# Four spectrum rows a block: one 1024-column product in place of two, and what storing them takes

## The chip, the cores and the metric

One Trainium2 chip; the program runs on one of its cores. The metric is the device time of one execution, in microseconds (us), lower is better. Three executions of the kernel before were timed, and one more was profiled. The engines are named as in the profile: PE is TensorE (PEld its weight loads), DVE is VectorE, ACT is ScalarE, POOL is GpSimd, and SP is the engine whose queue issues nearly all of the DMAs here.

## The reference, cut to what matters

One layer: a norm, a joint projection of 1024 tokens, three branches (Hyena long convolution, FNet, mLSTM), a merge and a mixture of experts. The change lies in the Hyena branch: the implicit filter is evaluated, turned into a spectrum, and multiplied with the spectrum of the signal, twice (order 0 and 1).

```python
def hyena_filter(L, lp):
    ...
    fwd, bwd = h[:, :, 0], h[:, :, 1]
    k = jnp.concatenate([fwd, jnp.zeros_like(fwd[:1]), jnp.flip(bwd[1:], axis=0)], axis=0)
    k = k * lax.rsqrt(jnp.sum(k * k, axis=0, keepdims=True) + EPS)
    return jnp.fft.rfft(k, axis=0)

def fft_longconv(u, kf, skip):
    L = u.shape[1]
    uf = jnp.fft.rfft(u, n=2 * L, axis=1)
    y = jnp.fft.irfft(uf * kf[None], n=2 * L, axis=1)[:, :L]
    return y + u * skip
...
    z = x1 * fft_longconv(v, kf[:, 0], skip[0])
    return x2 * fft_longconv(z, kf[:, 1], skip[1])
```

The product `uf * kf` is the complex product in question: re·re − im·im and re·im + im·re.

## The kernel before, in words

The transforms are matrix products with cosine and sine matrices, each float32 product done as three matmuls (`mm3`, lines L230 to L232) on a high and a low part of both factors; the parts come from a cast on ACT (L215) and a subtraction on DVE (L216). The program runs on one core as a line of stages, in us of the profiled span: about 0 to 200 start, conditioning and the filter's small network; 200 to 300 the **filter spectra**, interleaved with the projection; on to 650 the projection; then mLSTM and FNet; 880 to 1100 the **convolution**; merge, output and experts to the end.

`filt_spectra` goes over four kinds of spectrum in the order 2, 0, 1, 3 (kinds 0 and 1: real and imaginary part of the even frequencies, 2 and 3 of the odd ones), and in each over blocks of 128 frequencies (`fb`) and the two orders `o`. A kind loads its two folded filters (`kf<-pd`, 1 MB each) and the matrices (`fm`), splits them, and for each block and order runs a group of matmuls into PSUM (`pb`). From there come tiles `kk` of 128x512, in one of two ways: a block alone is copied out by ACT (L648); a pair of blocks is copied in one half by ACT (`ke`, L662) and combined by DVE to a sum (L664) and a difference (L665). Each tile is written to DRAM (`Kd`), L651 or L667. Row 0 of the first block of kind 0 carries two frequencies: in one place the halved value (L650) is wanted, in another a value that a small product gives (L627 to L631), which goes to a tensor of its own, `Kl` (L632). The tiles `kk` turn round in a ring of four buffers, so a fifth tile waits until the first one's write has landed.

In the convolution four passes (order, half of the channels) go over eight blocks each: four of even and four of odd frequencies (`par`, `fb`). `conv_fwd` makes a block's spectrum in PSUM (`p`, 128x2x256, real and imaginary), loads the filter's block with two DMAs (L956) and forms the product on DVE: one product with the tile as it is (L970), one with its two halves swapped (L971, a reversed view), a difference (L973), a sum (L974). In the first block of a pass (even, `fb` 0) the swapped tile is loaded by itself, with three DMAs: 128 rows (L966), rows 1 to 127 (L967), and row 0 from `Kl` (L968). `conv_inv` then transforms back, one block later.

Which instruction stands where on its engine is set by a scheduler when the kernel is built: from priorities, buffer rings and estimated durations it writes one fixed order for each engine, and each engine runs its list in that order. An instruction that waits holds up all that stand behind it on its engine; DMAs that SP issues stand in one such list, the filter's writes and the loads of the projection's weights alike.

Of the kernel before, what the change touches and what calls it, by code (L numbers as in the profile page):

```python
# [8 lines left out]
F32 = mybir.dt.float32  # L9
# [155 lines left out]
class Prog:  # L165
# [421 lines left out]
    def filt_spectra(self):  # L587
        nc = self.nc
        A = self.A

        self.Kd = self.dram([4, 4, 128, 2, 512], name="Kd")
        self.Kl = self.dram([1, 2, 512], name="Kl")

        skip = self.t("F2", "sk", 1, F32, (1, 2, 512))
        nc.sync.dma_start(skip.rearrange("p o c -> p (o c)"), self.skd.rearrange("i p -> (i p)").unsqueeze(0))
        for kind in (2, 0, 1, 3):
            kd, minus = {}, []
            for o in range(2):
                f = self.load("F2", "kf", 2, self.pd[o, kind].rearrange("k p c -> p k c"), (128, 4, 512))
                if kind < 2:  # L600

                    g, (a, b) = self.t("F2", "kf", 2, F32, (128, 4, 512)), (f[:, :2], f[:, 2:])
                    for i, sub in enumerate((kind == 1, kind == 0)):
                        (nc.vector.tensor_sub if sub else nc.vector.tensor_add)(g[:, 2 * i:2 * i + 2], a, b)
                    if kind == 0:
                        minus.append(self.t("F2", "kv", 2, F32, (1, 512)))
                        nc.vector.tensor_add(minus[o], g[0:1, 2, :], skip[:, o, :])
                        nc.sync.dma_start(g[0:1, 2, :], self.pv[o])
                        nc.vector.tensor_add(g[0:1, 2, :], g[0:1, 2, :], skip[:, o, :])
                        nc.vector.tensor_add(g[0:1, 0, :], g[0:1, 0, :], skip[:, o, :])  # L610
                    else:
                        nc.vector.tensor_copy(g[0:1, 2, :], f[0:1, 2, :])
                    f = g
                elif kind == 2:
                    nc.vector.tensor_add(f[0:1, 0, :], f[0:1, 0, :], skip[:, o, :])
                kd[o] = h, l = [self.t("F2", "kd" + x, 2, F32R, f.shape) for x in "hl"]
                for b in (0, 2):
                    self.split(h[:, b:b + 2], l[:, b:b + 2], f[:, b:b + 2])
            if kind == 0:
                p = self.ps("pb", (128, 2, 512))  # L620
                minus1 = self.t("F2", "sign", 1, F32R, (128, 2))
                nc.gpsimd.memset(minus1.bitcast(F32), -1.0)
                sign = self.onesr[:, :2], minus1
                for o in range(2):
                    h, l = kd[o]
                    for k in range(2):
                        nc.tensor.matmul(p[:2, o, :], sign[k], h[:, k, :], start=k == 0, stop=False)  # L627
                        nc.tensor.matmul(p[:2, o, :], sign[k], l[:, k, :], start=False, stop=k == 1)
                for o in range(2):
                    t = self.t("F2", "kk", 4, F32, (1, 512))  # L630
                    nc.vector.tensor_scalar(t, p[0:1, o, :], 0.5, None, op0=ALU.mult)  # L631
                    nc.sync.dma_start(self.Kl[:, o, :], t)  # L632
            for fb in (0, 2, 1) if kind < 2 else (0, 1):
                if kind == 0 and fb == 1:

                    for o in range(2):
                        self.split(kd[o][0][0:1, 0, :], kd[o][1][0:1, 0, :], minus[o])
                src = A["filt_odd"][kind - 2, fb] if kind > 1 else A["filt_even"][kind, fb]
                n = src.shape[1]
                mh, ml = self.parts("F2", "fm", 2, self.load("F2", "fm", 1, src, (128, n, 128)))  # L640
                if kind < 2 and fb < 2:
                    p = self.ps("pb", (128, 2, 512))
                    for o in range(2):
                        h, l = kd[o]
                        for k in range(2):
                            self.mm3(p[:, o, :], mh[:, k, :], ml[:, k, :], h[:, k, :], l[:, k, :], k == 0, k == 1)
                        kk = self.t("F2", "kk", 4, F32, (128, 512))
                        nc.scalar.copy(kk, p[:, o, :])  # L648
                        if kind == 0 and fb == 0:
                            nc.vector.tensor_scalar(kk[0:1], kk[0:1], 0.5, None, op0=ALU.mult)  # L650
                        nc.sync.dma_start(self.Kd[kind, fb, :, o, :], kk)  # L651
                    continue

                for o in range(2):
                    h, l = kd[o]
                    p = self.ps("pb", (128, 2, 512))
                    for i in range(2):
                        ks = [(k, k if kind > 1 else 2 + k) for k in range(i, n, 2)]
                        for k, kx in ks:
                            self.mm3(p[:, i, :], mh[:, k, :], ml[:, k, :], h[:, kx, :], l[:, kx, :], k == i, k == ks[-1][0])  # L660
                    e = self.t("F2", "ke", 1, F32, (128, 512))
                    nc.scalar.copy(e, p[:, 0, :])  # L662
                    kk = [self.t("F2", "kk", 4, F32, (128, 512)) for _ in range(2)]
                    nc.vector.tensor_add(kk[0], p[:, 1, :], e)  # L664
                    nc.vector.tensor_sub(kk[1], *((p[:, 1, :], e) if kind % 2 else (e, p[:, 1, :])))  # L665
                    for i in range(2):
                        nc.sync.dma_start(self.Kd[kind, fb + i * (2 if kind > 1 else 1), :, o, :], kk[i])  # L667
        if "kd" in self.dbg:
            nc.sync.dma_start(self.dbg["kd"], self.Kd)
            nc.sync.dma_start(self.dbg["kl"], self.Kl)  # L670
            nc.sync.dma_start(self.dbg["hnorm"], self.hnorm)


    def wblock(self, src):
# [234 lines left out]
    def conv_in(self, src, half, tiles=None, engines="vv"):  # L909


        nc = self.nc
# [16 lines left out]
        sh = (128, 2, 256)  # L929
        u2 = []  # L930
        for k in (0, 2, 1, 3):
# [6 lines left out]
            nc.scalar.copy(raw[k], p)  # L938
            if k >= 2:
                a, b = raw[k - 2], raw[k]  # L940
                e = [self.t("C", "t", 5, F32, sh) for _ in range(2)]
                nc.vector.tensor_add(e[0], a, b)
                nc.vector.tensor_sub(e[1], a, b)
                u2.append([self.parts("C", "u2", 4, e[i]) for i in range(2)])
        return u2, [raw[k] for k in range(4)]

    def conv_fwd(self, ut, o, half, par, fb):

        nc = self.nc
        cc = slice(256 * half, 256 * half + 256)  # L950
        if par and fb == 0:
            ut[1] = [self.parts("C1", "u1", 4, r) for r in ut[1]]
        p = self.ps("gp", (128, 2, 256))
        kk = self.t("C", "kk", 3, F32, (128, 2, 256))
        for im in range(2):
            nc.sync.dma_start(kk[:, im, :], self.Kd[2 * par + im, fb, :, o, cc])  # L956
            mh, ml = self.mat("f", par, im, fb)
            us = ut[1] if par else [u[im ^ (fb > 1)] for u in ut[0]]
            sg, nk = par ^ im, len(us)
            for k, (uh, ul) in enumerate(us):  # L960
                self.mm3(p[:, im, :], mh[:, k, :], ml[:, k, :], uh[:, sg, :], ul[:, sg, :], k == 0, k == nk - 1)
        sw = kk[:, ::-1, :]
        if par == 0 and fb == 0:

            sw = self.t("C", "t", 5, F32, (128, 2, 256))
            nc.sync.dma_start(sw[:, 0, :], self.Kd[1, 0, :, o, cc])  # L966
            nc.sync.dma_start(sw[1:128, 1, :], self.Kd[0, 0, 1:128, o, cc])  # L967
            nc.sync.dma_start(sw[0:1, 1, :], self.Kl[:, o, cc])  # L968
        t1, t2 = self.t("C", "t", 5, F32, (128, 2, 256)), self.t("C", "t", 5, F32, (128, 2, 256))
        nc.vector.tensor_mul(t1, p, kk)  # L970
        nc.vector.tensor_mul(t2, p, sw)  # L971
        y = self.t("C", "t", 5, F32, (128, 2, 256))
        nc.vector.tensor_sub(y[:, 0, :], t1[:, 0, :], t1[:, 1, :])  # L973
        nc.vector.tensor_add(y[:, 1, :], t2[:, 0, :], t2[:, 1, :])  # L974
        return self.parts("C", "y", 3, y)

    def conv_inv(self, acc, y, o, half, par, fb):


        nc = self.nc  # L980
# [17 lines left out]
        for g in range(2):  # L998
            for ct in range(2):
                i = 4 * o + 2 * half + ct  # L1000
                n, m = self.hnorm[:, i:i + 1], self.hnegn[:, i:i + 1]
                p = acc[0][g][ct]
                e = self.t("C1", "e", 1, F32, (128, 256))
                s = acc["s"][g][ct] = self.t("C1", "s", 4, F32, (128, 512))

                odd, even = (p[:, 256:], p[:, :256])[::1 if g == 0 else -1]
# [4 lines left out]
    def conv_out(self, acc, o, half, dst):  # L1011
# [7 lines left out]
        for part in range(2):  # L1019
            for ct in range(2):  # L1020
                i = 4 * o + 2 * half + ct
                if part == 0:
# [4 lines left out]
                    if o and half:  # L1027
                        nc.vector.scalar_tensor_tensor(s, acc[1][1][ct], n, s, op0=ALU.mult, op1=ALU.add)
                        continue
                    g = self.t("C", "t", 5, F32, (128, 512))  # L1030
                    nc.scalar.activation(g, acc[1][1][ct], AF.Copy, scale=n)
                    nc.vector.tensor_add(s, s, g)
                    continue
# [1126 lines left out]
```

## Time and profile before

| | |
|---|---|
| timed executions | 1688.49, 1693.48, 1694.13 us; median 1693.48 us |
| profiled execution | 1690.53 us, its span 1688.8 us |
| mean granted TensorE clock | 0.972 |
| busy shares of the span | PE 92%, DVE 71%, ACT 40%, POOL 19% |
| the chain that ended last | PE 73%, DVE 12%, DMA 8%, ACT 3% |

The busy shares are means over stages with different limits. The chain that ended last is followed back from the last instruction, from each instruction to what released it; a share of it tells on what kind of work the end of the program hung. The rows on which the argument rests are shown further down, in groups.

### The profile page before, as it was taken

How to read it: one execution, taken by the hardware profiler on the slowest of the kernel's cores; microseconds unless marked ns; L12 is line 12 of the kernel's file. 1: busy time of each engine (PE TensorE's matmuls, PEld its weight loads, DVE VectorE, ACT ScalarE, POOL GpSimd, SP SyncE). 2: the span in 40 equal slices, each digit the busy share in tenths (PEclk: the TensorE clock that was granted, in tenths of full speed). 3: DMA queues.
4: the chain of work that ended last, by engine and by line, in shares of the span. 5: the costliest groups of instructions: out<-in, count | busy, mean ns of one | idle time of the engine just before them, and what ended most of it. 6: DMA issues, size and time to landing. Idle time of an engine off the chain costs nothing.

```text
span 1688.8 us, 22676 instructions
## 1 busy us (share of the span) xinstructions
PE 1559.7 (92%) x8473; PEld 1300.7 (77%) x8473; DVE 1191.5 (71%) x1849; ACT 678.7 (40%) x1029; POOL 315.7 (19%) x282
## 2 busy tenths in 40 slices
PE   3999999999999999899989888899999969999993
PEld 1488877788888887778877777778878859999992
DVE  5689775966776869788645988864255567776776
ACT  4475545433222124444324433332033354554553
POOL 0000000000000001000002200125623354465651
PEclk9999999999999999999999999999999969999997
DMA  7544566422222365976435323585463388999984
GB/s 267 178 138 175 206 218 227 150 81 83 100 112 82 131 256 172 315 259 226 155 128 168 122 100 105 187 304 190 156 227 113 137 247 245 307 286 278 278 228 172
DMA packets 124355, 317.03 MB, mean 188 GB/s; under 512 B 18009, under 2 KB 40529, under 8 KB 124242
## 3 DMA queue, kind: packets, MB, share of 16 engines
q1 hardware_dynamic: 111562, 278.72, 47.8%
q0 software_dynamic: 10496, 32.36, 7.8%
q10 hardware_dynamic: 2184, 4.47, 0.7%
q8 instruction: 68, 1.11, 0.3%
q14 instruction: 45, 0.37, 0.1%
HBM read 226.49 MB, written 89.01 MB: 187 GB/s over the span
## 4 chain that ended last, share of the span: by engine, by line
PE 73%; DVE 12%; DMA 8%; ACT 3%; issue 3%; POOL 1%; SPq 0%; ACTq 0%; POOLq 0%; DVEq 0%
PE gp L230 12%; PE gp L231 11%; PE gp L232 11%; PE pb L230 8%; PE pb L232 8%; PE pb L231 8%; PE ph L230 2%; PE ph L232 2%; PE ph L231 2%; PE q L344 2%; DMA t<-Kl 1%; PE pb L1734 1%; DVE t L971 1%; DMA w<-sum 1%; DVE t L970 1%
## 5 line engine op out<-in xcount | busy, mean ns | idle before, releaser
L230 PE MATMUL gp<-ht,wh 128*128 128x512 f32 x784 | 310.6, 396 | 2.7 <-ACT wh L215 1.6
L232 PE MATMUL gp<-ht,wl 128*128 128x512 f32 x784 | 308.7, 394 | 0.9 <-DVE wl L216 0.9
L231 PE MATMUL gp<-ht,wh 128*128 128x512 f32 x784 | 309.0, 394 | 0.0
L230 PEld LDWEIGHTS gp<-ht,wh 128*128 128x128 f32 x784 | 148.4, 189 | 37.0 <-issue 2.3
L232 PEld LDWEIGHTS gp<-ht,wl 128*128 128x128 f32 x784 | 148.2, 189 | 31.7 <-DVE wl L216 1.3
L231 PEld LDWEIGHTS gp<-ht,wh 128*128 128x128 f32 x784 | 148.3, 189 | 30.9 <-DVE r L526 0.9
L230 PE MATMUL pb<-xh,gh 128*128 128x224 f32 x512 | 142.8, 279 | 0.0
L232 PE MATMUL pb<-xh,gl 128*128 128x224 f32 x512 | 141.8, 277 | 0.0
L231 PE MATMUL pb<-xl,gh 128*128 128x224 f32 x512 | 140.7, 275 | 0.0
L723 DVE SCALAR_TENSOR_TENSOR u<-z,hy_cw,u 128x945 f32<-128x945 f32 (+2 forms) x96 | 117.3, 1221 | 13.5 <-ACT u L715 11.3
L216 DVE TENSOR_TENSOR wl<-w,wh 128x1024 fp32r<-128x1024 f32 x57 | 70.4, 1235 | 63.5 <-ACT wh L215 63.1
L215 ACT CAST wh<-w 128x1024 fp32r<-128x1024 f32 x57 | 59.8, 1048 | 128.8 <-PE gp L231 82.0
L230 PEld LDWEIGHTS pb<-xh,gh 128*128 128x128 f32 x512 | 99.3, 194 | 0.3 <-ACT xh L215 0.2
L231 PEld LDWEIGHTS pb<-xl,gh 128*128 128x128 f32 x512 | 99.3, 194 | 0.1
L232 PEld LDWEIGHTS pb<-xh,gl 128*128 128x128 f32 x512 | 99.2, 194 | 0.0
L723 DVE SCALAR_TENSOR_TENSOR u<-z,ml_cw,u 128x945 f32<-128x945 f32 (+2 forms) x64 | 77.9, 1220 | 26.0 <-ACT u L715 24.9
L708 ACT ACTIVATE z<-gp,b_cols 128x512 f32<-128x512 f32 x48 | 32.8, 684 | 139.0 <-PE gp L232 139.0
L216 POOL TENSOR_TENSOR ml<-m,mh 128x512 fp32r<-128x512 f32 x24 | 34.9, 1454 | 194.8 <-ACT mh L215 191.6
L873 POOL MEMSET z<- 128x1024 f32 x1 | 1.0, 960 | 364.3 <-DVE u L723 364.3
L708 ACT ACTIVATE z<-gp,bh 128x512 f32<-128x512 f32 x46 | 31.6, 686 | 87.6 <-PE gp L232 74.7
L1690 POOL DMA_INDIRECT sum<-y,sidx x26 | 45.4, 1745 | 80.5 <-DVE y L1799 76.8
L1718 DVE TENSOR_TENSOR gl<-x,gh 128x1024 fp32r<-128x1024 f32 x33 | 40.4, 1230 | 28.1 <-ACT gh L1716 28.1
(608 smaller groups left out, 3972.6 us busy)
## 6 DMA issues: line engine op xcount, KB each, us to landing
w<-in_ada_rest SPq DMA_DIRECT2D x32, 512.0 KB
w<-in_w_gu SPq DMA_DIRECT2D x32, 512.0 KB
x<-in_w_gu SPq DMA_DIRECT2D x32, 512.0 KB
w<-in_w_gate SPq DMA_DIRECT2D x24, 512.0 KB
g<-gd SPq DMA_DIRECT2D x24, 512.0 KB
gd<-z SPq DMA_DIRECT2D x23, 512.0 KB
r<-in_ada_in SPq DMA_DIRECT2D x16, 512.0 KB
pd<-ft SPq DMA_DIRECT2D x32, 256.0 KB
```

The costliest lines, as they stand in the source:

```text
L215: self.copied = nc.scalar.copy(hi, src)
L216: return (nc.vector if eng == "v" else nc.gpsimd).tensor_sub(lo, src, hi.bitcast(F32))
L230: mm(ps, lh, rh, start=start, stop=False)
L231: mm(ps, lh, rl, start=False, stop=False)
L232: mm(ps, ll, rh, start=False, stop=stop)
L344: nc.tensor.matmul(p, c[:, kk, :], x[:, 512 * j:512 * j + 512], start=kk == 0 and x is ws[0], stop=kk == 7)
L708: return lambda s, p: self.nc.scalar.activation(z[:, s], p, func, bias=bias, scale=scale)
L723: last = nc.vector.scalar_tensor_tensor(ui[:, r0:r1, c0:c1], zi[:, r0 + dy:r1 + dy, c0 + dx:c1 + dx], taps[:, i:i + 1], ui[:, r0:r1, c0:c1 ...
L970: nc.vector.tensor_mul(t1, p, kk)
L971: nc.vector.tensor_mul(t2, p, sw)
L1690: return self.nc.gpsimd.indirect_dma_start(out=out, out_offset=bass.IndirectOffsetOnAxis(ap=ix, axis=0), in_=src, in_offset=None, **kw)
L1718: lo = (nc.vector if engines[i] == "v" else nc.gpsimd).tensor_sub(ml, m, mh.bitcast(F32))
```

## The change

Every block's spectrum is kept in DRAM as four rows of 256 for each half of the channels: re, −im, im, re. A function `keep` writes each `kk` tile twice, a real tile to rows 0 and 3, an imaginary one to row 2, and, negated by ACT into a further tile of the same ring, to row 1. Each write takes 128 rows of two pieces of 256. For kind 0, block 0, the write to row 3 leaves out row 0 of the frequencies (127 rows), since there the value that went to `Kl` before is written, now into `Kd` itself. In the convolution a block's four rows come with one DMA (128x1024), one DVE operation multiplies them with the spectrum in PSUM, read twice by a broadcast view, and one addition of 512 columns makes real and imaginary part of the product. The three extra loads of the first block are gone, and so is `Kl`. The ring `t` of the convolution goes from five tiles to four, and the small tile `e` moves into it.

```diff
-        self.Kd = self.dram([4, 4, 128, 2, 512], name="Kd")
-        self.Kl = self.dram([1, 2, 512], name="Kl")
+        self.Kd = self.dram([2, 4, 128, 2, 2, 4, 256], name="Kd")
+        def keep(kk, kind, fb, o):
+            par, im = divmod(kind, 2)
+            d = lambda i, a=0: self.Kd[par, fb, a:, o, :, i, :]
+            v = kk.rearrange("p (h c) -> p h c", h=2)
+            if not im:
+                nc.sync.dma_start(d(0), v)
+                a = int(kind == 0 and fb == 0)
+                nc.sync.dma_start(d(3, a), v[a:])
+                return
+            nc.sync.dma_start(d(2), v)
+            kn = self.t("F2", "kk", 4, F32, (128, 512))
+            nc.scalar.mul(kn, kk, -1.0)
+            nc.sync.dma_start(d(1), kn.rearrange("p (h c) -> p h c", h=2))
...
-                    nc.sync.dma_start(self.Kl[:, o, :], t)
+                    nc.sync.dma_start(self.Kd[0, 0, 0:1, o, :, 3, :], t.rearrange("p (h c) -> p h c", h=2))
...
-                        nc.sync.dma_start(self.Kd[kind, fb, :, o, :], kk)
+                        keep(kk, kind, fb, o)
...
-                        nc.sync.dma_start(self.Kd[kind, fb + i * (2 if kind > 1 else 1), :, o, :], kk[i])
+                        keep(kk[i], kind, fb + i * (2 if kind > 1 else 1), o)
...
-                e = [self.t("C", "t", 5, F32, sh) for _ in range(2)]
+                e = [self.t("C", "t", 4, F32, sh) for _ in range(2)]
...
-        kk = self.t("C", "kk", 3, F32, (128, 2, 256))
+        kk = self.t("C", "kk", 3, F32, (128, 2, 2, 256))
+        nc.sync.dma_start(kk.rearrange("p a b c -> p (a b) c"), self.Kd[par, fb, :, o, half])
         for im in range(2):
-            nc.sync.dma_start(kk[:, im, :], self.Kd[2 * par + im, fb, :, o, cc])
...
-        sw = kk[:, ::-1, :]
-        if par == 0 and fb == 0:
-            sw = self.t("C", "t", 5, F32, (128, 2, 256))
-            nc.sync.dma_start(sw[:, 0, :], self.Kd[1, 0, :, o, cc])
-            nc.sync.dma_start(sw[1:128, 1, :], self.Kd[0, 0, 1:128, o, cc])
-            nc.sync.dma_start(sw[0:1, 1, :], self.Kl[:, o, cc])
-        t1, t2 = self.t("C", "t", 5, F32, (128, 2, 256)), self.t("C", "t", 5, F32, (128, 2, 256))
-        nc.vector.tensor_mul(t1, p, kk)
-        nc.vector.tensor_mul(t2, p, sw)
-        y = self.t("C", "t", 5, F32, (128, 2, 256))
-        nc.vector.tensor_sub(y[:, 0, :], t1[:, 0, :], t1[:, 1, :])
-        nc.vector.tensor_add(y[:, 1, :], t2[:, 0, :], t2[:, 1, :])
+        nc.vector.tensor_mul(kk, kk, p.unsqueeze(1).to_broadcast([128, 2, 2, 256]))
+        y = self.t("C", "t", 4, F32, (128, 2, 256))
+        nc.vector.tensor_add(y, kk[:, :, 0, :], kk[:, :, 1, :])
...
-                e = self.t("C1", "e", 1, F32, (128, 256))
+                e = self.t("C", "t", 4, F32, (128, 256))
```

In the changed file `keep` lies on L595 to L606 (the writes to rows 0, 3, 2 and 1 on L599, L601, L603 and L606, the negation on L605). Three places show how the fixed orders move.

SP's queue, kinds 0 and 1, the changed kernel: `kk_990` and `kk_1001` are the two orders of the block with the 127-row write, `kk_1021` to `kk_1039` the pairs after it, `fm_1101` and `kf_1089` loads for kind 1.

```order
L599 DMA Kd_803<-kk_990 128x2x256
L601 DMA Kd_803<-kk_990 127x2x256
L601 DMA Kd_803<-kk_1001 127x2x256
L599 DMA Kd_803<-kk_1021 128x2x256
L599 DMA Kd_803<-kk_1001 128x2x256
...
L220 DMA fm_1101<-in_filt_even 128x256
L599 DMA Kd_803<-kk_1038 128x2x256
L601 DMA Kd_803<-kk_1038 128x2x256
...
L220 DMA kf_1089<-pd_457 128x4x512
```

Where one write of 128x512 stood for each tile, two stand now, and two of them have 127 rows; the loads for the next kind are behind them.

PE's list where the filter spectra end, before: `pb_1263` is the last group of the filter, `gp_2207` and `gp_2233` are parts of the projection (10 and 24 matmuls here), `gp_2298` the first product that takes the weights `wvh`.

```order
L232 MATMUL pb_1263<-kdh_1182,fml_1239 128x512
L232 MATMUL gp_2207<-ht_345,wl_2203 128x512
...
L230 MATMUL gp_2233<-ht_381,wh_2202 128x512
L231 MATMUL gp_2233<-ht_382,wh_2202 128x512
L232 MATMUL gp_2233<-ht_381,wl_2203 128x512
L230 MATMUL gp_2298<-wvh_2276,htch_444 128x512
```

The same place in the changed kernel, where `pb_1320` is the filter's last group and `gp_2361` the first product with `wvh`:

```order
L231 MATMUL pb_1320<-kdl_1222,fmh_1289 128x512
L232 MATMUL pb_1320<-kdh_1221,fml_1290 128x512
L230 MATMUL gp_2361<-wvh_2339,htch_444 128x512
L231 MATMUL gp_2361<-wvl_2340,htch_444 128x512
```

The 34 matmuls that stood between are now ahead of the filter's last groups: counting the rows of matmuls in PE's list, the last one of the filter is the 1026th and was the 992nd. Likewise the first matmul of the kind-0 block 0 (`pb_983`, before `pb_976`) is the 773rd and was the 729th, and the first of kind 1 (`pb_1107`, before `pb_1092`) the 869th and was the 820th.

ACT's list at the same end, in the changed kernel: `ke_1333` is the copy of the last pair, `kk_1335` and `kk_1336` its two tiles, `u` belongs to the mLSTM's small convolution.

```order
L677 COPY ke_1333<-pb_1320 128x512
L605 ACTIVATE kk_1313<-kk_1308 128x512
L605 ACTIVATE kk_1317<-kk_1309 128x512
L605 ACTIVATE kk_1340<-kk_1335 128x512
L605 ACTIVATE kk_1344<-kk_1336 128x512
L726 ACTIVATE u_2253<-z_2200,ml_cb_1354,ml_cw_1352 128x1024
L726 ACTIVATE u_2325<-z_2269,ml_cb_1354,ml_cw_1352 128x1024
L215 CAST wvh_2339<-w_2337 128x1024
```

The negations stand between the last copy and the casts of the weights that PE needs next; no negation stood there before. On DVE, at the start of kind 0, the split `kdl_939` of kind 0's filter now stands ahead of the tile `kk_897` of kind 2, whose counterpart was ahead of it before.

## Rows read from the trace of the kernel before

**Rows 1.** The page: busy time by engine, and the chain that ended last.

```profile
PE 1559.7 (92%) x8473; PEld 1300.7 (77%) x8473; DVE 1191.5 (71%) x1849; ACT 678.7 (40%) x1029; POOL 315.7 (19%) x282
...
PE 73%; DVE 12%; DMA 8%; ACT 3%; issue 3%; POOL 1%; SPq 0%; ACTq 0%; POOLq 0%; DVEq 0%
```

**Rows 2.** Windows, filter spectra: length, PE, PEld, DVE, ACT, POOL busy, PEclk, DMA share, GB/s.

```profile
220.00:230.00 10.00, 8.00 (x36) 5.93 (x36) 5.99 (x9) 2.19 (x4) 0.00 (x0) 1.00 0.70 240
230.00:240.00 10.00, 10.00 (x38) 7.92 (x37) 7.58 (x11) 4.53 (x7) 0.00 (x0) 0.83 0.37 140
...
300.00:310.00 10.00, 8.09 (x34) 5.94 (x34) 10.00 (x10) 5.08 (x6) 0.00 (x0) 1.00 0.68 198
```

**Rows 3.** The chain of waits, 190 to 330 us: start, length, work or DMA.

```profile
220.01 7.30 DMA Kd<-kk
...
245.03 1.14 DMA Kl<-kk
...
272.23 7.44 DMA kf<-pd
...
303.11 4.42 DMA w<-in_w_qk
...
308.65 0.50 PE gp L230
```

**Rows 4.** The timeline of SP's queue, end of the filter spectra.

```profile
287.79 8.87 SPq L667 DMA_DIRECT2D Kd<-kk  x8
```

**Rows 5.** The timeline of DVE, last pairs: start, length, in brackets the idle time before.

```profile
292.29 0.69 DVE L664 TENSOR_TENSOR kk<-pb,ke 128x512 f32<-128x512 f32 x1 [1.45 <-ACT ke L662]
...
295.02 0.69 DVE L664 TENSOR_TENSOR kk<-pb,ke 128x512 f32<-128x512 f32 x1 [1.44 <-ACT ke L662]
```

**Rows 6.** The timeline of ACT: the first copy of kind 0 block 0, and the end.

```profile
243.04 0.59 ACT L648 COPY kk<-pb 128x512 f32<-128x512 f32 x1
...
297.21 1.23 ACT L715 ACTIVATE u<-z,ml_cb,ml_cw 128x1024 f32<-128x1024 f32 x1
298.35 1.98 ACT L215 CAST wvh<-w 128x1024 fp32r<-128x1024 f32 x2
```

**Rows 7.** The timeline of PE: a matmul of kind 1, and the filter's last.

```profile
256.14 0.39 PE L231 MATMUL pb<-kdl,fmh 128*128 128x512 f32 x1
...
293.92 0.40 PE L232 MATMUL pb<-kdh,fml 128*128 128x512 f32 x1
294.15 0.39 PE L232 MATMUL gp<-ht,wl 128*128 128x512 f32 x1
```

**Rows 8.** The chain of waits, 870 to 1110 us (the convolution).

```profile
954.40 7.33 DMA t<-Kl
...
977.28 1.13 DVE u L1038
...
993.72 2.05 DMA kk<-Kd
...
1001.40 8.80 DMA t<-Kl
```

**Rows 9.** The waits of DVE, 945 to 1075 us: total, times, longest.

```profile
DVE t L971 <- DMA t<-Kl: 11.9, 3, 5.3
```

**Rows 10.** Windows, a stretch of the second pass (columns as in rows 2).

```profile
965.00:992.00 27.00, 21.12 (x136) 18.62 (x137) 25.48 (x49) 8.25 (x15) 0.00 (x0) 0.87 0.33 117
```

**Rows 11.** The timeline of DVE, one block's product.

```profile
998.92 0.69 DVE L970 TENSOR_TENSOR t<-gp,kk 128x512 f32<-128x512 f32 x1
999.52 0.68 DVE L971 TENSOR_TENSOR t<-gp,kk 128x512 f32<-128x512 f32 x1
1000.12 0.68 DVE L216 TENSOR_TENSOR yl<-t,yh 128x512 fp32r<-128x512 f32 x1
1000.72 0.42 DVE L973 TENSOR_TENSOR t<-t 128x256 f32<-128x256 f32 x1
1001.05 0.42 DVE L974 TENSOR_TENSOR t<-t 128x256 f32<-128x256 f32 x1
```

More of the change, by code (lines that the diff above doesn't have):

```diff
@@ L666, in filt_spectra @@
                     for i in range(2):
-                        nc.sync.dma_start(self.Kd[kind, fb + i * (2 if kind > 1 else 1), :, o, :], kk[i])
[L668 to L671, printed above, removed]
+                        keep(kk[i], kind, fb + i * (2 if kind > 1 else 1), o)
     def wblock(self, src):
@@ L949, in conv_fwd @@
         nc = self.nc
-        cc = slice(256 * half, 256 * half + 256)
         if par and fb == 0:
@@ L1029, in conv_out @@
                         continue
-                    g = self.t("C", "t", 5, F32, (128, 512))
+                    g = self.t("C", "t", 4, F32, (128, 512))
                     nc.scalar.activation(g, acc[1][1][ct], AF.Copy, scale=n)
```

## The prediction

> **What bounds the kernel now.** I read the page first: PE is busy 92% of the span and makes 73% of the chain that ended last, DVE 12% [rows 1]. Then the two stretches that the change touches, by windows, and in each the chain and the timelines.
>
> In the filter spectra PE is the bound. A window of 10 us has 10.00 us of PE, except where the stage hiccups: 8.00 in one window, after which the granted clock is 0.83 for the next, and 8.09 in 300 to 310 [rows 2]. The chain says why: at 220.01 the ring of four `kk` tiles waits 7.30 us for a write, at 303.11 a weight load takes 4.42, and PE goes on at 308.65 [rows 3]. So writes and loads already touch the bound here; whatever delays PE in this stage is lost, since the projection behind it keeps PE full.
>
> In the convolution DVE is the bound: in a stretch of 27 us it works 25.48, PE 21.12 [rows 10]. At the start of three passes DVE waits for row 0 of the swapped tile, 11.9 us in all [rows 9], and the chain goes through that load, 7.33 and 8.80 us for a single row [rows 8].
>
> About 0.3% (5 us) is what a measurement of this kernel can tell from no change.
>
> **Filter, term 1: the two 127-row writes.** The price of a row comes from the load just named. It stands in SP's queue right behind the load of 127 rows of 1 KB. A 2 KB row alone, `Kl<-kk`, lands after 1.14 us [rows 3]; behind the 127 rows it takes 7.33 to 8.80 [rows 8]. The difference, 6.2 to 7.7 us, says that the 127 rows go one after another, 0.049 to 0.060 us each, where 128 rows loaded normally take 2.05 in all [rows 8]. A new write has 127x2 rows of 1 KB: 254 x 0.049 = 12.4 us, and two of them on the same engine 24.8.
>
> When: the first tile of that block was copied at 243.04 [rows 6]; it now stands 44 matmuls later, at 0.23 us each (293.92 to 294.15) [rows 7], so 253.2, and the copy's 0.59 makes 253.8. The first write is through at 266.2, the second at 278.6. Behind them: `kk_1039`, whose buffer is the second tile's, and the matrix `fm_1101` (its share on the busy engine). DVE runs in order, so behind `kk_1039` (0.7) stand three splits of 1024 columns at 1.13 (the nearest row of that width [rows 8]): 282.7. PE needs the last of them for kind 1. Kind 1 began at 256.14 [rows 7], now stands 49 matmuls later (11.3 us), and needs that split 10 matmuls further on (2.3): 269.7. Loss **13 us**. Bounds: 0, if the rows are spread or covered; 19, with 0.060 a row.
>
> The Trainium skill ("DMA: Bandwidth & Descriptors", the section on why a DMA increments its semaphore by 16, "How many engines") says that the number of engines is the largest up to 16 that divides the slowest dimension of both patterns, and gives 1 for 127 partitions. No row of this case shows a 127-row write with two pieces a row. By the rule its 254 pieces stay on one engine and the sum is mine; were the pieces counted instead, two engines would share them, and the sum is the first rival's.
>
> **Term 2: the ring.** 34 tiles become 50 in the same four buffers (16 negated ones), and each is held by one or two writes. A pair's turn now takes all four. With nothing in the way it is 0.69 on DVE [rows 5] and 2.05 for a transfer (the nearest unloaded one, a load [rows 8]): 2.74, against 2.73 between two pairs now [rows 5]. That costs nothing; behind a 1 MB filter load, as at 220.01, it is 0.69 + 7.30 [rows 3], 5.3 more. Two such loads (7.44 at 272.23 [rows 3]) stand among kind 1's writes: 0 to 10.5; I take one turn, **5**, since between them stand matmuls of the projection that cover the other. The 16 negations (0.59 each, by the copy of that size [rows 6]) and 32 more issues on SP lie beside PE's work, ACT being busy half the time [rows 2]; where they don't is the next term.
>
> **Term 3: the end.** Eight writes there took 8.87 us of SP's time beside PE [rows 4], and behind the last filter matmul stood 34 matmuls of the projection, 7.8 us, as cover. In the new order they are earlier (not lost, they fill PE there) and the cover is gone: PE waits for copy 0.59 [rows 6], sum and difference 0.69 each [rows 5], negation 0.59, two `u` of 1.23 and a cast of 0.99 [rows 6], together 6.0, plus the ring for the last pair, a turn of 2.74. Less the 1.9 that PE idled there before [rows 2]: 6.8, taken as **7**. Bounds: 4 (no ring wait) and 12 (a loaded transfer, 7.44).
>
> **Term 4: the early wait.** With `kdl` of kind 0 ahead of the waiting tile, the 2.0 us of idle PE and the low clock (0.17 of 10 us) [rows 2] may go: 0 to 3.7, taken **−3**.
>
> **Convolution, term 5.** A block's product takes 0.60 + 0.60 + 0.33 + about 0.34 by the spacing of starts [rows 11], 1.87; the new one 1.13 for 1024 columns [rows 8] and 0.60 for 512: 1.73. 32 blocks give 4.5 us; the three waits, 11.9 [rows 9]. Of these 16.4 some comes back: a block now comes as one load of 512 KB, 4.42 [rows 3] instead of 2.05 [rows 8], three buffers deep, and PE is not far below DVE [rows 10]. Taken **−12**, bounds −4 and −16.4. The loads' 7 MB more lie in a stretch with a DMA share of 0.33 [rows 10], so they cost nothing by volume. The smaller `t` ring has two fewer tiles a block to hold: nothing.
>
> **Sum:** 13 + 5 + 7 − 3 − 12 = +10 us on the profiled execution's 1690.5: 1700.5. That execution lies 3 us under the median of 1693.5, so against the median **1703.5**.
>
> **The rivals.**
>
> *The long writes share two engines (0.16).* Each takes 6.2, the second is through at 266.2, before kind 1 begins at 267.4: term 1 is 0, the rest stays, −3: 1690.5. For it: 254 pieces. Against it: the only row of such a transfer shows no spreading.
>
> *The filter hides it all (0.17), faster.* The price of a row is that of a load; a write may hold its engine less. The point from which it decides: from 253.8 to kind 1 there are 13.6 us for 508 rows, so under 0.027 us a row term 1 is nothing. With the projection's matmuls pulled ahead also covering the ring, the end at 4, and terms 4 and 5: 4 − 3 − 12 = −11: 1682.5. For it: PE's list is full of independent work. Against: the ring was already on the chain at 220.01 [rows 3].
>
> *The convolution gives little (0.13).* The wide product reads PSUM through a broadcast view, which no row shows; if it costs two of 0.60, and the 512 KB load becomes the wait at a pass's start, term 5 is −4: +18, 1711.5. That the change does not do what it says would look like this too. Against: one row of the changed list does a block's 1024 columns.
>
> *Everything in the filter at its upper end (0.06):* 19 + 10.5 + 12 − 15 = +26.5: 1720.
>
> **How the numbers follow.** The forecast has 0.48 (own range 1697 to 1711). Faster than 1688.4: the second rival and a third of the first, 0.22. Within 0.3%: the rest of the first and the foot of the forecast, 0.16. Slower: 0.62. The range from 1683 to 1719 leaves out the last rival and the lower half of the second.
>
> **What would show it.** In the changed profile: idle PE before the kind-1 groups until about 282, behind `Kd<-kk` or `fm`; no PE work between the filter's last group and the first with `wvh` for some 8 us; no 0.83 window at 230; in the convolution no `t<-Kl`, one DVE product of about 1.1 us and a sum of 0.6 a block, and passes some 3 to 4 us shorter. Wrong would be a full PE in 265 to 285 (term 1), a resumption at the end without a gap (term 3), or DVE waiting for `kk<-Kd` in each pass (term 5).

## The result and the profile after

| | before | after |
|---|---|---|
| timed executions, median (range) | 1692.68 (1688.49 to 1694.13), 4 runs | 1716.67 (1715.93 to 1718.79), 4 runs |
| ratio, with 95% interval | | 1.0153 [1.0137, 1.0169] |
| span of the profiled execution | 1688.8 | 1717.0 |
| mean granted TensorE clock | 0.972 | 0.961 |

The kernel is 24 us slower where 10 were forecast; 1716.67 lies near the upper end of the range that was given. The span of the profiled execution grew by 28.2 us. In it the convolution got shorter about as forecast, and the filter spectra lost far more than I had summed.

Windows of the kernel after, filter spectra (length; busy time of PE, PEld, DVE, ACT, POOL with counts; PEclk; DMA share; GB/s), which answer to [rows 2]:

```profile
220.00:230.00 10.00, 10.00 (x45) 7.62 (x44) 6.33 (x10) 2.23 (x4) 0.00 (x0) 1.00 0.91 313
230.00:240.00 10.00, 10.00 (x46) 8.29 (x45) 4.50 (x7) 4.14 (x6) 0.00 (x0) 1.00 0.83 277
...
260.00:270.00 10.00, 0.00 (x0) 0.00 (x0) 0.69 (x1) 0.00 (x0) 0.00 (x0) 0.75 0.07 24
270.00:280.00 10.00, 0.83 (x2) 0.73 (x3) 2.06 (x3) 1.47 (x2) 0.00 (x0) 0.50 0.67 222
...
300.00:310.00 10.00, 6.68 (x30) 5.05 (x28) 3.78 (x5) 5.92 (x9) 0.00 (x0) 0.97 0.87 294
310.00:320.00 10.00, 5.45 (x12) 3.65 (x13) 3.05 (x3) 4.97 (x8) 0.00 (x0) 0.50 0.62 192
...
330.00:340.00 10.00, 1.51 (x7) 0.97 (x5) 5.07 (x6) 6.76 (x10) 0.00 (x0) 0.66 0.94 301
```

The early hiccup is gone: 220 to 240 hold 91 matmuls instead of 74, 17 x 0.23 = 3.9 us won. Then PE stands still for nearly 20 us with the data engines at 0.07 of their time, and comes up short twice more, with data engines that are busy. After a stop the granted clock is 0.50 for a while (270 to 280, 310 to 320), the lower of its two levels (1.2 GHz), and matmuls follow each other at 0.43 us instead of 0.23.

The chain of waits of the kernel after (start, length, what), which answers to [rows 3]:

```profile
251.22 14.47 DMA Kd<-kk
265.81 0.70 DVE kk L679
266.51 4.61 SPq L599
271.22 0.56 SPq L599
271.84 6.67 DMA Kd<-kk
278.53 0.59 ACT kk L663
279.17 0.80 PE pb L230
...
303.47 5.38 DMA Kd<-kk
...
330.28 2.40 DMA Kd<-kk
...
333.43 2.36 DMA Kd<-kk
...
348.78 0.50 PE gp L230
```

PE goes on with the projection at 348.78, in the kernel before at 308.65 [rows 3]: the filter lost 40.1 us. About the difference to the span's 28.2 came back in the convolution. Its first product and the split behind its last output, in the chain of the kernel before:

```profile
912.25 0.66 DVE t L970
...
1098.61 1.15 DVE y2l L216
```

From start to start that is 186.4 us. In the chain of the kernel after:

```profile
953.64 1.21 DVE kk L972
...
1127.52 1.23 DVE y2l L216
```

That is 173.9 us, 12.5 less; the waits on a load of `t` are gone from DVE's list of waits.

The 127-row writes, in the DMA view of the kernel after, 252 to 272 us (40 slices; busy tenths, then GB/s):

```profile
DMA  8000000000000000000000000000000000000007
GB/s 301 8 6 2 4 10 25 25 25 25 23 25 25 25 25 23 25 25 25 25 23 25 25 25 25 23 25 25 25 25 23 25 25 25 25 23 25 25 25 254
DMA packets 693, 0.69 MB, mean 35 GB/s; under 512 B 17, under 2 KB 693, under 8 KB 693
```

25 GB/s at a share of 0.07, about one sixteenth: one engine works, the others have nothing. The first of the two writes lands at 265.69, 14.47 us after its issue (its pieces flow at that rate only from about 255 on), the second at 276.44. Between the two landings lie 10.75 us for 254 pieces of 1 KB, 0.042 us each, which is the 25 GB/s. What I had not seen coming stands in the groups of the lines that issue the writes (min/median/max in ns of one issue on SP):

```profile
L601 SPq DMA_DIRECT2D Kd<-kk x16: 303/530/6605, 220.8 to 283.1; - x16
...
L599 SPq DMA_DIRECT2D Kd<-kk x16: 359/432/10679, 220.3 to 282.7; - x16
```

Two issues took 6.6 and 10.7 us: that of the second long write, and that of the plain write behind it. SP itself stood still. But that is not what made the writes behind it late. In the trace the semaphore of the plain write whose issue took 10.7 us has fifteen of its sixteen counts by 273.05 and the last one at 277.13, 0.69 us behind the end of the second long write. The next two plain writes are complete at 277.82 and 278.51, again 0.69 us apart, and 16 pieces, a sixteenth of such a write, make 0.68 us at 0.042. So each had a part on the busy engine, in line behind the long writes; issued earlier, it would have stood in the same line.

The waits of ACT and PE, 205 to 345 us (total, times, longest):

```profile
PE pb L230 <- ACT kk L663: 24.2, 3, 19.4
...
ACT kk L663 <- DMA Kd<-kk: 20.4, 1, 20.4
```

ACT waits for a buffer of the ring. The tile in it is one of the pair whose writes stand behind the long ones, and its second write is complete only at 278.51. PE waits for the PSUM that ACT does not empty. The group of matmuls that stands still is the last one of kind 0, nine matmuls ahead of kind 1's first.

### The profile page after: what moved, and what is told of

Same layout as the page of the kernel before. It is cut to its first block, busy times and chain, and to the rows that moved or that the text cites. A ratio compares the mean times of both kernels' runs of the same rounds, so it can differ in the third digit from the quotient of the medians.

```text
span 1717.0 us, 22632 instructions
## 1 busy us (share of the span) xinstructions
PE 1564.2 (91%) x8473; PEld 1307.2 (76%) x8473; DVE 1187.6 (69%) x1785; ACT 688.0 (40%) x1045; POOL 314.3 (18%) x282
## 4 chain that ended last, share of the span: by engine, by line
PE 72%; DVE 11%; DMA 8%; ACT 3%; issue 3%; SPq 1%; POOL 1%; ACTq 0%; POOLq 0%; DVEq 0%
PE gp L230 11%; PE gp L231 11%; PE gp L232 11%; PE pb L230 8%; PE pb L232 8%; PE pb L231 7%; DMA Kd<-kk 2%; PE ph L230 2%; PE ph L232 2%; PE q L344 2%; PE ph L231 2%; PE pb L1734 1%; DVE kk L972 1%; DVE t L974 1%; PE pb L1365 1%
```

## The experiments

Fifteen kernels, in comparison with the kernel before on the same chip; 0.0059 of a ratio is 10 us. Each is named in words.

**The writes cut: 112 and 15 rows in place of 127.**

```diff
-                nc.sync.dma_start(d(3, a), v[a:])
+                if a:
+                    nc.sync.dma_start(d(3)[1:113], v[1:113])
+                    nc.sync.dma_start(d(3)[113:], v[113:])
+                    return
+                nc.sync.dma_start(d(3), v)
```

> The changed kernel with each of the two 127-row writes cut into one of 112 rows and one of 15. Theory A (the 254 pieces of such a write go through one engine, SP's queue stands still behind them, and PE stopped for 19.45 us at 259.7): the stop goes, about 20 us less, 1694 to 1700 us, no issue of a write longer than 1.5 us, PE busy over 8 in 260 to 280. Rival B (it is the doubled volume of the writes that delays everything): less than 6 us gained, over 1710.

Ratio 1.0062 [1.0037, 1.0086], against 1.0153 for the change: 15 us. In the spans it is 1699.1 against 1717.0, and PE goes on at 329.94 instead of 348.78, 18.8 earlier. Windows of this run:

```profile
260.00:280.00 20.00, 20.00 (x89) 16.14 (x88) 8.09 (x10) 8.29 (x13) 0.00 (x0) 1.00 0.83 263
280.00:300.00 20.00, 9.68 (x32) 6.43 (x31) 8.48 (x10) 10.28 (x16) 0.00 (x0) 0.79 0.84 272
...
310.00:320.00 10.00, 1.23 (x6) 0.69 (x4) 4.00 (x6) 6.62 (x11) 0.00 (x0) 0.76 0.98 317
```

The stop is gone, and with it nothing else: the later holes stay.

**The long writes alone**, in the kernel before (two writes of 127 rows of two pieces, to a tensor that nobody reads):

```diff
+                        if kind == 0 and fb == 0:
+                            nc.sync.dma_start(self.Kx[1:, o, :, 3, :], kk.rearrange("p (h c) -> p h c", h=2)[1:])
```

> The kernel before plus two writes of 127 rows of two pieces (the same tiles as in the change, to a tensor that nobody reads) and nothing else. Theory A (two such writes alone stop SP's queue and then PE): 13 to 20 us slower than the kernel before; one engine's 25 GB/s for some 22 us in the DMA view, an issue of a write of 6 us or more on SP. Rival (they cost only since the rest of the changed filter stands behind them): under 6 us.

Ratio 1.0112 [1.0088, 1.0136], 19 us. The timeline of SP's queue in this run (start, length):

```profile
246.88 9.26 SPq L654 DMA_DIRECT2D Kx<-kk  x2
256.24 10.26 SPq L670 DMA_DIRECT2D Kd<-kk  x1
266.59 0.66 SPq L652 DMA_DIRECT2D Kd<-kk  x1
```

The first row holds the issues of both long writes; the second of them lasts 6.56 us by itself. The third row's write is a plain one of 128 rows, and so is the second's, whose issue takes 10.26 us. Two long writes make the loss by themselves. That SP's standstill is a part of it is not shown: as in the changed kernel, the second long write is complete at 272.08, and the plain writes behind it at 272.73, 273.38 and 274.02, in line on the one engine.

**No negated tile** (with the cut writes; −im stored as im, the convolution's sum of 512 becomes a difference and a sum of 256):

```diff
-            kn = self.t("F2", "kk", 4, F32, (128, 512))
-            nc.scalar.mul(kn, kk, -1.0)
-            nc.sync.dma_start(d(1), kn.rearrange("p (h c) -> p h c", h=2))
+            nc.sync.dma_start(d(1), v)
```

> As the run with the cut writes, and the row -im is stored as im: no negation on ACT, no further tile in the ring, as many writes and bytes as the changed kernel; in the convolution the sum of 512 becomes a difference and a sum of 256 (0.67 instead of 0.60 us a block, 2.3 us in all). Theory A (the negated tiles in the ring of four and the negations ahead of the weight casts make the rest of the filter's loss, some 24 us before 350): another 12 to 20 us less than with the cut writes alone, 1677 to 1686. Rival B (volume): the loss stays, within 5 us of the run with the cut writes alone.

Ratio 1.0057 [1.0039, 1.0074]: nothing against the cut writes alone. In the trace PE goes on with the projection at 326.78 instead of 329.94, and the longer sums in the convolution cost 2.3 us by the durations, so the filter gained 3 us where 12 to 20 were expected. My theory of the rest fell here. The ring's and the negations' waits left the chain and others took their place.

**Pieces of 2 KB** (with the cut writes; the store laid out with 512 channels together, `[2, 4, 128, 2, 4, 512]`). D1 and D2 are the volume of the writes and the number of issues on SP, set out with the next run:

> The run with the cut writes, with the store laid out so that a row's 512 channels lie together: each write has one piece of 2 KB a row as before instead of two of 1 KB, the loads of the convolution stay at pieces of 1 KB. D3, pieces: 8 to 20 us less than the run with the cut writes. D1 and D2: within 4 us of it.

Ratio 1.0045 [1.0029, 1.006], 3 us under the cut writes, with overlapping intervals. Not the pieces.

**The second writes on POOL** (with the cut writes; rows 3 and 1 by `nc.gpsimd.dma_start`):

> The run with the cut writes, with the second write of every tile (rows 3 and 1) issued by POOL instead of SP; bytes, pieces and ring as there. What is left of the filter's loss there (PE goes on at 330 instead of 309) has three theories. D1, volume: the engines that move the data are near full (0.83 to 0.98 of their time) and loads wait behind writes: within 5 us of the run with the cut writes. D2, SP's queue: 32 more issues stand in order ahead of the loads of the next kind and of the weights: 8 to 20 us less than the run with the cut writes.

Ratio 1.0038 [1.0022, 1.0054], 4 us less than the cut writes: within D1's bound, and no more than a hint for D2. By the trace 32 matmuls of the projection stand behind the filter's last group again (34 in the kernel before, none in the change), and yet PE goes on only at 327.31, 18.7 us later than before. So taking the second writes out of SP's list does not by itself bring the filter's loss back.

**Two rows stored, loaded twice** (the convolution's product as in the change, the filter as before except for a whole tensor for the special row):

```diff
+        for i, r in enumerate((re, im_, im_, re2)):
+            nc.sync.dma_start(kk[:, i // 2, i % 2, :], r)
...
+        nc.vector.tensor_mul(kk, kk, p.unsqueeze(1).to_broadcast([128, 2, 2, 256]))
```

> The convolution as in the change (one product of 1024), the filter as before: two rows stored, the four rows of the tile come with four 128 KB loads in the convolution, the special row as in the run with the whole row tile; no row -im, so a difference and a sum of 256 (0.67 instead of 0.60). All of D1 to D3: the filter's loss is gone, the convolution's gain stays, 10 to 15 us faster than the kernel before and within 3 us of the run with the whole row tile. Rival: without the wide load the four loads a block make DVE wait and half of the convolution's gain goes: 3 to 8 us faster than before.

Ratio 0.9935 [0.991, 0.9961], 11 us faster than before. Without second writes there is no filter loss. This is the ground for the next five runs, which put single parts of the filter's change back.

**A small second write** of each tile, 16 rows:

```diff
+                        nc.sync.dma_start(self.Kx[kind, fb, :16, o, :], kk[:16])
```

> The run with two rows loaded twice, and each tile of the filter written a second time, but only 16 of its 128 rows, to a tensor that nobody reads: as many writes in SP's queue and as many landings for the ring as in the run without the negated tile, an eighth of the second bytes; PE's list has lost its projection matmuls behind the filter's last group, as in the changed kernel. D1 (volume of the second writes): within 4 us of the run with two rows loaded twice. D2 (the number of DMAs, and the order of the engines' lists that the scheduler makes of them): 12 to 20 us slower than that run.

Ratio 1.0036 [1.0015, 1.0057]: 17 us lost to 32 small writes. The chain of this run, where PE stops after 280 (start, length, what; the SPq rows are issues):

```profile
284.38 0.70 DVE kk L669
285.10 0.32 SPq L672
285.47 0.46 SPq L673
286.02 0.37 SPq L672
286.44 0.43 SPq L673
286.92 2.17 DMA fm<-in_filt_even
289.11 0.41 ACT fmh L215
289.56 0.78 PE pb L230
```

The first write waits for its tile, the others for nothing, and the load behind them lands after 2.17 us. It is late since it stands behind four writes in SP's list, and PE has nothing else to do, since the projection's matmuls were placed ahead. Of the 34 that stood behind the filter's last group before, this run's list, like the changed kernel's, has none.

**The whole second write**, 128 rows:

> As the run with the small second write, with all 128 rows. D1 and D2: 12 to 20 us slower than the run with two rows loaded twice; D1 says that this run is far slower than the small second write, D2 that the two are alike within 4 us.

Ratio 1.0063 [1.0045, 1.0082], 4.6 us more than the small one by the ratios. The intervals overlap.

**The negated tiles alone** (in ring and ACT, with 16 writes of 16 rows on SP):

> The run with two rows loaded twice, and for each imaginary tile a negated tile in the same ring of four, made by ACT and written with 16 of its rows to a tensor that nobody reads; no other second write. If the negated tiles cost by themselves (ring, and ACT ahead of the casts): 5 to 12 us slower than the run with two rows loaded twice. If they cost only beside the second writes' loss: within 4 us.

Ratio 0.9979 [0.9962, 0.9996], 7.4 us slower than the ground. So they cost something without the other second writes. Whether that is ring and ACT is not shown, since this run also has 16 further writes in SP's list, and 32 such writes cost 17 us above. The loss does not add to that of the second writes: the run without negated tiles, above, gained nothing in the times.

**The small second write on POOL:**

```diff
-                        nc.sync.dma_start(self.Kx[kind, fb, :16, o, :], kk[:16])
+                        nc.gpsimd.dma_start(self.Kx[kind, fb, :16, o, :], kk[:16])
```

> The run with the small second write, with that second write issued by POOL instead of SP: as many DMAs, bytes and landings for the ring; PE's list again has 33 projection matmuls behind the filter's last group, as in the run with two rows loaded twice. If the loss of the small second write lies in SP's list and in what the scheduler makes of it (loads behind writes, PE's cover pulled ahead): within 5 us of the run with two rows loaded twice, 8 to 14 us faster than the kernel before. If it lies in the second landing that each tile of the ring waits for, or in the number of transfers as such: slower than the kernel before by 3 us or more.

Ratio 0.9926 [0.9902, 0.9951]. The 17 us are gone, with as many transfers, bytes and landings. The loss lies in SP's list and in the order that all the lists take with it. Which of the two was not separated: in both runs the loads stand elsewhere in SP's list and the projection's matmuls elsewhere in PE's.

**The whole second write on POOL:**

> The same with all 128 rows in the second write, issued by POOL; the lists of PE and SP are those of the run with the small second write on POOL. If volume costs by itself: 8 us or more slower than that run. If not: within 4 us of it.

Ratio 1.0001 [0.9988, 1.0014], 12.7 us slower than the small one, with the order on every engine the same in the two traces. Volume costs after all once the lists don't hide it. Its chain shows where:

```profile
263.62 7.93 DMA fm<-in_filt_even
...
279.67 4.20 DMA Kx<-kk
...
287.21 7.92 DMA fm<-in_filt_odd
```

The same two loads in the chain of the run with the small second write on POOL:

```profile
261.34 4.08 DMA fm<-in_filt_even
...
278.30 6.96 DMA fm<-in_filt_odd
```

The loads take 3.9 and 1.0 us longer beside the bytes, and a tile of the ring waits for its second write, which the other chain does not have. PE goes on at 323.55 instead of 310.94.

**All writes on POOL** (the change with the cut writes):

> The change with the 127-row writes cut into 112 and 15 rows and all writes of the filter's tiles issued by POOL, the rest as in the change (four rows, negated tiles, one load of 512 KB, one product, one sum). If SP's list is what was left of the filter's loss: 8 to 14 us faster than the kernel before, some 35 less than the changed kernel, PE's cover behind the filter's last group back. If the negated tiles keep costing as in the run with them alone: 4 to 8 us less of it, 0 to 6 us faster than before.

Ratio 0.9954 [0.9939, 0.9969]: 8 us faster than before, and 34 faster than the changed kernel. Against the run with the second writes alone on POOL it is 14 us: the place of the first writes counts as well, with the order that all the lists take with it. PE goes on at 318.67, still 10.0 us later than before. Whether that is the bytes, the negated tiles or both was not tried.

**The old product** on the changed store:

```diff
+        if par == 0 and fb == 0:
+            sw = self.t("C", "t", 5, F32, (128, 2, 256))
+            nc.sync.dma_start(sw, self.Kd[par, fb, :, o, half, 2:4, :])
+        t1, t2 = self.t("C", "t", 5, F32, (128, 2, 256)), self.t("C", "t", 5, F32, (128, 2, 256))
+        nc.vector.tensor_mul(t1, p, kk)
+        nc.vector.tensor_mul(t2, p, sw)
```

> The changed kernel with its filter as it is, and the convolution's product as before (two products of 512, difference and sum of 256, five t tiles, two loads a block); the first block's swapped tile comes from the rows im and re of the new store with one 128-row load. Theory A (of the convolution's 12.5 us most came from the three waits on the one-row load, 11.9, and little from the wider product, 4.5 by the durations): 2 to 6 us slower than the changed kernel, 1719 to 1723, and DVE has no wait on a load of t over 1 us. Rival C (the wider product makes the gain): 10 or more slower, 1727 and up.

Ratio 1.0201 [1.017, 1.0232], 8 us over the change, between the two expectations. But by its trace the convolution is no longer: from the first product at 953.7 to the split behind the last output at 1128.0, 174.3 us against 173.9. From the first product to the last the change takes 162.4 us and this run 166.6, so the wide product won the 4.2 that the durations promised (4.5); from the last product to that split the change takes 11.5 and this run 7.7, so nearly all of it went again. The span is 4.2 over the change's, nearly all of it behind the convolution, which this edit does not touch. What the rest of the 8 us is stays open.

**A whole tensor for the special row**, in the kernel before:

```diff
-            nc.sync.dma_start(sw[1:128, 1, :], self.Kd[0, 0, 1:128, o, cc])
-            nc.sync.dma_start(sw[0:1, 1, :], self.Kl[:, o, cc])
+            nc.sync.dma_start(sw[:, 1, :], self.Kl[:, o, cc])
```

> The kernel before with one thing changed: the first block's special row is kept as a whole tensor of 128 rows (written in 112 and 15 rows beside row 0), so that the swapped tile comes with two 128-row loads instead of a 128-, a 127- and a 1-row load. Theory A: the three waits of 11.9 us go, nothing else moves: 1680 to 1685, faster than both kernels. Rival C: the waits were no loss since PE or the next transform ends last anyway: within 4 us of the kernel before, 1689 or more.

Ratio 0.9938 [0.9918, 0.9958], 10.5 us faster than before. The waits on the three-part load were most of the convolution's gain of 12.5.

**An outer product** on top of it (`kk` and `p` both broadcast, two rows stored, no load added; the first block of a pass as before):

```diff
+            nc.vector.tensor_mul(t, kk.unsqueeze(2).to_broadcast([128, 2, 2, 256]),
+                                 p.unsqueeze(1).to_broadcast([128, 2, 2, 256]))
+            nc.vector.tensor_sub(y[:, 0, :], t[:, 0, 0, :], t[:, 1, 1, :])
+            nc.vector.tensor_add(y[:, 1, :], t[:, 0, 1, :], t[:, 1, 0, :])
```

> The run with the whole row tile, and in all blocks but the first of a pass one outer product of 1024 columns (both factors broadcast, no further loads, two rows stored), then a difference and a sum of 256: 1.13 + 0.67 = 1.80 instead of 1.87 us a block. By the durations 2 us less than the run with the whole row tile, so 10 to 15 us faster than the kernel before. Rival: broadcasting both factors is dearer than one: no gain, or slower than the run with the whole row tile.

Ratio 0.989 [0.9864, 0.9916], 1674.22 us: 19 us faster than the kernel before and the best of all. Its products, by the groups of DVE:

```profile
L974 DVE TENSOR_TENSOR tt<-kk,gp 128x1024 f32<-128x1024 f32 x28 | 34.0, 1213 | 1.6 <-PE gp L232 1.4
```

1213 ns with both factors broadcast, as long as the change's product with one:

```profile
L972 DVE TENSOR_TENSOR kk<-kk,gp 128x1024 f32<-128x1024 f32 x32 | 38.6, 1214 | 4.7 <-PE gp L232 4.7
```

The gain over the whole-row run is 8 us, more than the 2 by durations; the `t` ring and the place of `e` changed along with it, and these were not tried apart.

## Why the prediction was wrong, point by point

- **The step that failed** is in terms 2 and 3: together they put 12 us on what is left of the filter's loss without the long writes, and that came to 25. The second writes were set at nothing there, both as 32 issues on SP ("beside PE's work") and as bytes beside the next loads, and so were the matmuls that had moved ahead ("not lost"). The runs showed 17 us for 32 small second writes in SP's list, with the order of the lists that goes with them, and 12.7 us for the bytes of whole second writes with the lists alike. Term 1 was too small besides.
- **What bounds the kernel**: right. What PE lost in the filter was lost for good, and DVE bound the convolution.
- **Term 1 (13 us)**: the mechanism, all pieces of both long writes in line on one engine, was right, the size too small. The cut writes showed 18.8 us in the trace and 15 in the times, the long writes alone 19. I let PE come to kind 1 at 267.4 and wait there from 269.7 on, for the third split behind `kk_1039` on DVE. (Kind 1's first matmul before is at 255.45; the one of [rows 7], from which I counted, is 0.7 later.) That split came nearly as forecast, done at 282.35, forecast 282.7. But PE stopped earlier, at 259.7, since I had not followed the ring to ACT: the tile of kind 0's last block needs a buffer, too, and until ACT has copied it the next group has no PSUM. That wait ended at 279.17. The price of a piece was 0.042 us, under the 0.049 that I took from the load.
- **One engine or two**: the trace shows one (25 GB/s, a share of 0.07), so the first rival is out. The rule of the Trainium skill ("DMA: Bandwidth & Descriptors", "How many engines", in the section on why a DMA increments its semaphore by 16), one engine for 127 partitions, holds here for a write with two pieces a row, too.
- **Terms 2 and 3 (12 us)**: with the long writes cut, PE goes on 21.3 us late in spite of 3.9 us won early, so they were 25. The matmuls that had moved ahead were not lost, but bunched ahead they covered nothing when the next kind's matrix came late, and I costed only the last of the places. The 8.87 us of [rows 4] were no price of issues either: that row runs from the first to the last of eight issues of some 0.32 us. The small second write has the 32 issues and almost none of the bytes, and costs 17 us; on POOL it costs nothing. The negated tiles, on which I had built term 2, cost 7 us when they are alone, with 16 writes of their own, and next to nothing on top of the rest. The parts do not add up, and how the 25 us divide between the lists, the bytes and the negated tiles stays open.
- **Term 4 (−3)**: right, −3.9.
- **Term 5 (−12)**: right, 12.5. To the last product the convolution is 15 us shorter, near the 16.4 of product and waits, and some of it came back behind the last product, as assumed. The larger part is the waits: 10.5 us without the wide product. The wide load was no new wait.
- **The rivals**: the one on the other side, that the filter hides it all, is out. The upper-end case gave 1720, with terms 1 to 3 at 41.5 together, and had 0.06. It was nearest: PE went on 40.1 us late, 44 with the 3.9 won early. I had treated the upper ends as independent; whether they have a cause in common is not shown.

## What to carry to other kernels

A DMA of 127 rows is not only slow itself: here it ran on one engine, each write issued behind it had a part in line on that engine, and so buffers stayed held and ACT and PE stopped. Look for such loads as well as writes. Here a special row that was loaded with a 127-row and a 1-row DMA cost 10 us, and the repair of that alone beat both kernels. When an edit adds DMAs to a queue in which the next stage's loads stand, compare the new lists place by place, since the scheduler here answered with another order of the whole stage. Cost what stands behind the new DMAs and what is left to cover a late load, not only the issues, and cost the bytes as well.

## What the runs showed that I had not expected

- An issue on SP lasted 6.6 and 10.7 us in the change, and 6.56 and 10.26 in the run with the long writes alone, each behind one or two writes of 254 pieces, where the median of the lines with plain writes is 0.32 to 0.53. The wait shows as the issue's own length, not as a wait for a semaphore; the tiles that these writes take were there. That the engine's queue had no room left may be the reason; it was not tried with other numbers of pieces. By the landings above, the writes behind were not later for it.
- A product that reads PSUM and SBUF through broadcast views costs what a plain one of that width does: 1213 and 1214 ns, against 1214 for the plain product `u` of 128x1024 (L1038) before.
